# Pairs of four-block transposes of the attention probabilities issued as one visit of TensorE, and a new table of priorities

## The chip, the cores and the metric

The kernel runs on one core of a Trainium2 chip. The metric is the time of the whole program on the device in microseconds (us), as the median of the runs shown. The profile is one execution of the program, taken by the hardware profiler. Engines are named as in the profile: PE (TensorE's matmuls), PEld (its weight loads), DVE (VectorE), ACT (ScalarE), POOL (GpSimd) and SP (the queue that issues nearly all DMAs).

## What is computed

One hybrid decoder layer for a sequence of 2048 tokens and a model width of 1024, in float32. Cut to what matters here:

```python
h = rmsnorm(x, norm_pre_g)
z = einsum('bsd,de->bse', h, w_in)               # 1024 -> 4096 columns
q, k, v, g_attn, c_h, c_b, c_c, g_conv = split(z)
q, k = rope(q), rope(k)                          # 12 heads of 64
for window, dilation in ((128, 1), (512, 4), (2048, 16)):
    o_i, lse_i = dilated_window_attn(q, k, v, window, dilation)
o = sum(softmax(lse) * o_i)                      # mixed by the softmax denominators
attn_out = o * silu(g_attn)
conv_out = c_b * causal_depthwise_conv(c_c * c_h, conv_w) * silu(g_conv)
y = einsum('bse,ed->bsd', concat(attn_out, conv_out), w_out)
out = x + rmsnorm(y, norm_post_g)
```

## The kernel before

The 2048 tokens are cut into four blocks of 512. The input projection runs in 8 groups of 512 columns: groups 0 and 7 feed the convolution, groups 1 to 6 feed one pair of heads each. A group and a block together are a unit; 24 of the 32 units are attention units (`attn_unit`; in the text "the third unit" is the third of these 24, that is pair 0, block 2). Every float32 product is made as three products of rounded parts (`w.ap[:, 0]`, `w.ap[:, 1]`: main part and rest), so a projection step is the three matmuls L933 to L935 into one PSUM bank `z`.

An attention unit does the following. Rotary and scaling on DVE and POOL (L623, L627) with halves swapped by DMA (L611). Scores in two kinds, 4 (the dilated windows) and 1 (the near window): L691 and L719 multiply on halves of 64 rows of TensorE, two heads side by side, into banks `st`. DVE adds the mask and takes the row extreme (L698 for kind 4, L726 for kind 1), ACT takes the exponential (L702, L730). The probabilities `p` then lie with queries on partitions and must be transposed 128 by 128 for the product with v. `parts(h, kind, blk)` does that for up to four blocks: TensorE transposes them into one bank `st` (L759, a matmul against the identity in `cst`), ACT casts the bank to the main part (L764), DVE subtracts to get the rest (L765); both go to one of three buffers `pt`. `times` multiplies by v (L781), `gather` evacuates the result (L797 to L799). For kind 1, and for kind 4 in the first two blocks, a head has 4, 7 or 8 blocks; the loop calls `parts` on four blocks, then `times`, then `parts` on the next four. In the blocks 2 and 3 the far part of kind 4 is transposed on DVE (L750) instead, and the near part, four blocks at a time, as above.

The two kinds are weighted by their softmax denominators: the extremes and sums `e` travel to DRAM and back by small DMAs (L847 `ed<-e`, L849 `ex<-ed`), and DVE begins the weights with L857 to L859 (called the weights step below) as soon as its queue comes to them and `ex` has landed.

The order on every engine is made on the host by `Plan`: each operation has an engine, an estimated duration, a priority and the tiles it reads and writes; `schedule` plays the program through and each engine takes the ready operation of lowest priority number. Operations of TensorE have a mode (0 plain, 1 scores, 2 transposes); while an engine is in mode 1 or 2, a ready operation with a mode is taken before a plain one, so transposes that are ready together are issued together anyway. `SHIFT` moves the priority of single groups of operations, by stage and place in the code. The engines then execute their instructions strictly in this order, so an instruction that waits holds back all that stands behind it on its engine.

The banks are 3 named `z` and 5 named `st`; `st` serves scores, transposes and products with v alike. The loop that the change rewrites:

```python
for i in range(0, len(bl), 4):
    where = parts(h, kind, bl[i:i + 4])
    for half in range(2):
        part = {ac: v for ac, v in where.items() if ac[0] // 2 == half}
        if part:
            times(h, kind, part, O[half])
```

Of the kernel before, what the change touches and what calls it, by code (L numbers as in the profile page):

```python
# [32 lines left out]
ALU = mybir.AluOpType  # L33
# [77 lines left out]
class Op:  # L111
# [3 lines left out]


SHIFT = {
# [5 lines left out]
}  # L123


# [205 lines left out]
def hybrid_layer(ctx: ExitStack, tc: tile.TileContext, x, w_in, w_out, conv_w, g_pre, g_post,  # L331
# [257 lines left out]
    def attn_unit(n, p, b, zs):  # L589
# [144 lines left out]
                    ps + [(P[h, 1], "hold") for h in range(2)], rest)  # L734


        def parts(h, kind, blk, far=False):
            pt, m, pp = Tok(pt_r), len(blk), P[h, kind]
            tiles = sorted({a for a, _ in blk})
            if far:  # L740

                def src():
                    return pp.ap[:, tiles[0]:tiles[-1] + 1, 0:(b - 1) * 128]

                def dst(l):
                    return pt.ap[:, :m, l].rearrange("p (a c) q -> p a c q", c=b - 1)

                def cut(a):
                    return a.rearrange("p a (c q) -> p a c q", q=128)
                add("DVE", dvet(m * 128) + 0.05, pr, lambda: vec.transpose(src(), src()), w=[(pp, a) for a in tiles])  # L750
                add("ACT", actt(m * 128), pr + URG, lambda: act.copy(dst(0), cut(src())), r=[(pp, a) for a in tiles], w=[(pt, 0)])
                add("DVE", dvet(m * 128), pr + URG, lambda: vec.tensor_tensor(dst(1), cut(src()), f(dst(0)), op=ALU.subtract),
                    r=[(pp, a) for a in tiles] + [(pt, 0)], w=[(pt, 1)], port=True)
            else:
                ps = Tok(st_r)

                def tr():
                    for i, (a, c) in enumerate(blk):
                        nc.tensor.transpose(ps.ap[:, i * 128:(i + 1) * 128], pp.ap[:, a, c * 128:(c + 1) * 128], ident)  # L759
                add("PE", 0.111 * m, pr, tr, r=[(pp, a) for a in tiles] + ["cst"], w=[ps, (pt, "hold")], mode=2)  # L760

                def p4():
                    return ps.ap[:, :m * 128].rearrange("p (i c) -> p i c", c=128)
                add("ACT", actt(m * 128, True), pr + URG, lambda: act.copy(pt.ap[:, :m, 0, :], p4()), r=[ps], w=[(pt, 0)])  # L764
                add("DVE", dvet(m * 128), pr + URG, lambda: vec.tensor_tensor(  # L765
                    pt.ap[:, :m, 1, :], p4(), f(pt.ap[:, :m, 0, :]), op=ALU.subtract), r=[ps, (pt, 0)], w=[(pt, 1)])
            return {ac: (pt, i) for i, ac in enumerate(blk)}


# [43 lines left out]
        for kind in (4, 1):  # L813
            for h in range(2):
                if kind == 4:
                    bl = [(r, j) for r in range(4) for j in range(b + 1)]
                else:
                    bl = [(g, s) for g in range(4) for s in range(2) if not (b == 0 and g == 0 and s == 0)]
                if h == 0:
                    UU[kind] = Tok(uu_r), Tok(uu_r)  # L820
                O = [Tok(st_r), Tok(st_r)]
                if kind == 4 and b > 1:
                    where = {}
                    for half in range(2):
                        rs = range(2 * half, 2 * half + 2)
                        if b == 3 or half == 0:
                            where.update(parts(h, 4, [(r, c) for r in (rs if b == 3 else range(4)) for c in range(b - 1)], True))
                        where.update(parts(h, 4, [(r, c) for r in rs for c in (b - 1, b)]))
                        times(h, 4, {ac: v for ac, v in where.items() if ac[0] in rs}, O[half])
                else:  # L830
                    for i in range(0, len(bl), 4):
                        where = parts(h, kind, bl[i:i + 4])
                        for half in range(2):
                            part = {ac: v for ac, v in where.items() if ac[0] // 2 == half}
                            if part:
                                times(h, kind, part, O[half])
                for half in range(2):
                    gather(h, kind, half, O[half])
                if h == 1:
                    a, t = UU[kind]  # L840
                    add("POOL", poolt(C), pr, lambda a=a, t=t: pool.tensor_tensor(a.ap, a.ap, t.ap, op=ALU.add), r=[t], w=[a], port=True)  # L841
# [364 lines left out]
```

## Time and profile before

| what | number |
|---|---|
| median of three runs | 1198.13 us (1196.64 to 1198.43) |
| the profiled execution: its time, its span from first to last instruction | 1198.13 us, 1196.3 us |
| PE busy, matmuls | 1182.5 us (99%), 6716 |
| PEld busy | 981.9 us (82%) |
| DVE busy | 922.5 us (77%) |
| ACT busy | 716.1 us (60%) |
| POOL busy | 265.2 us (22%) |
| DMA queue q1's packets, share of 16 engines | 72.3% |

The busy time of PE overstates its work: a matmul's record includes the pipeline's depth, so records overlap. The work is better read from the distance between the starts of two matmuls that follow each other. The profiled execution took as long as the median of the runs.

### The profile page before, as it was taken

What the parts mean: (1) busy time and instruction counts of PE and PEld (TensorE: products, weight loads), DVE (VectorE), ACT (ScalarE), POOL (GpSimd) and SP (SyncE); (2) the same over time, 40 slices, a digit from 0 to 9 for tenths busy, and PEclk for the clock granted to TensorE, in tenths of its full rate; (3) what the DMA queues carried; (4) which work ended last, traced back from release to release, by engine and by line L of the source; (5) the groups of instructions that cost most, each with busy time, mean ns of one, the idle gap of its engine ahead of it and who ended that gap; (6) DMA issues with size and microseconds to landing.
All of it is one profiled execution on the core that took longest, in us unless ns stands there. A gap on an engine that the chain in (4) does not pass through costs nothing.

```text
span 1196.3 us, 20842 instructions
## 1 busy us (share of the span) xinstructions
PE 1182.5 (99%) x6716; PEld 981.9 (82%) x6716; DVE 922.5 (77%) x2331; ACT 716.1 (60%) x1875; POOL 265.2 (22%) x212
## 2 busy tenths in 40 slices
PE   9999999999999999999999999999999999999997
PEld 7788888888888888888878888888888888888886
DVE  4665478787779977786878867798877899787876
ACT  7433457656757676675857766576767563454443
POOL 0011123322223232222332232232332213100000
PEclk9999999999999999999999999999999999999999
DMA  9989766786768867777768777778657978635452
GB/s 342 371 324 360 247 217 213 251 245 221 213 212 261 255 203 238 215 239 216 231 214 246 235 217 228 222 250 274 225 168 228 318 225 335 203 124 192 139 172 89
DMA packets 175294, 280.46 MB, mean 234 GB/s; under 512 B 53712, under 2 KB 109776, under 8 KB 175184
## 3 DMA queue, kind: packets, MB, share of 16 engines
q1 hardware_dynamic: 174896, 278.86, 72.3%
q8 instruction: 53, 0.87, 0.3%
q14 instruction: 57, 0.47, 0.1%
q10 hardware_dynamic: 288, 0.27, 0.1%
HBM read 215.42 MB, written 51.05 MB: 223 GB/s over the span
## 4 chain that ended last, share of the span: by engine, by line
PE 87%; DMA 5%; DVE 3%; ACT 2%; issue 1%; SPq 1%; DVEq 0%; ACTq 0%
PE z L933 17%; PE z L935 16%; PE z L934 16%; PE st L781 8%; PE st L759 5%; PE st L691 4%; PE st L719 3%; PE st L1100 3%; PE st L1099 3%; PE st L1101 3%; PE z L1101 2%; PE z L1099 2%; PE z L1100 2%; DMA ex<-ed 1%; PE st L933 1%
## 5 line engine op out<-in xcount | busy, mean ns | idle before, releaser
L933 PE MATMUL z<-xt,w 128*128 128x512 f32 x960 | 391.0, 407 | 0.7 <-DVE rp L558 0.4
L935 PE MATMUL z<-xt,w 128*128 128x512 f32 x960 | 376.1, 392 | 0.0
L934 PE MATMUL z<-xt,w 128*128 128x512 f32 x960 | 375.5, 391 | 0.2 <-DVE xt L493 0.2
L933 PEld LDWEIGHTS z<-xt,w 128*128 128x128 f32 x960 | 180.7, 188 | 39.4 <-issue 7.5
L935 PEld LDWEIGHTS z<-xt,w 128*128 128x128 f32 x960 | 180.1, 188 | 39.9
L934 PEld LDWEIGHTS z<-xt,w 128*128 128x128 f32 x960 | 180.9, 188 | 29.7 <-DVE xt L493 0.5
L702 ACT ACTIVATE p<-p,sm 128x128 f32<-128x128 f32 (+3 forms) x192 | 105.7, 553 | 64.1 <-DVE sm L698 64.1
L781 PEld LDWEIGHTS st<-pt,v 128*128 128x128 f32 x852 | 118.2, 190 | 17.4 <-DVE pt L765 4.5
L781 PE MATMUL st<-pt,v 128*128 128x256 f32 x852 | 128.1, 286 | 3.4 <-DVE pt L765 3.2
L765 DVE TENSOR_TENSOR pt<-st,pt 128x512 fp32r<-128x512 f32 (+1 forms) x180 | 116.7, 675 | 16.6 <-ACT pt L764 14.9
L799 DVE TENSOR_TENSOR uu<-st,uu 64x256 f32<-64x256 f32 x192 | 79.5, 420 | 58.4 <-ACT uu L798 44.9
L797 ACT COPY uu<-st 64x256 f32<-64x256 f32 x192 | 69.5, 367 | 66.0 <-PE st L781 55.8
L764 ACT CAST pt<-st 128x512 fp32r<-128x512 f32 (+1 forms) x180 | 98.3, 579 | 14.6 <-PE st L759 12.1
L841 POOL TENSOR_TENSOR uu<-uu 128x512 f32<-128x512 f32 x48 | 69.3, 1443 | 158.8 <-DVE uu L799 139.3
L730 ACT ACTIVATE p<-p,e 128x256 f32<-128x256 f32 (+1 forms) x192 | 94.7, 497 | 15.8 <-DVE e L726 15.8
L698 DVE CUSTOM_DVE_ANT_0 p<-st,cst 128x128 f32<-128x128 f32 (+3 forms) x192 | 81.9, 486 | 28.1 <-PE st L691 27.7
L759 PE MATMUL st<-cst,p 128*128 128x128 f32 x708 | 98.3, 273 | 0.0
L759 PEld LDWEIGHTS st<-cst,p 128*128 128x128 f32 x708 | 82.5, 140 | 11.8 <-issue 1.2
L623 POOL TENSOR_TENSOR rp<-rp,cs 128x512 f32<-128x512 f32 x24 | 36.2, 1509 | 216.7 <-DMA rp<-rp 96.0
L798 ACT COPY uu<-st 64x256 f32<-64x256 f32 x192 | 68.7, 367 | 18.6 <-PE st L781 13.2
L726 DVE CUSTOM_DVE_ANT_0 p<-st,cst 128x256 f32<-128x256 f32 (+1 forms) x192 | 66.9, 410 | 13.9 <-PE st L719 13.6
L623 DVE TENSOR_TENSOR rp<-rp,cs 128x512 f32<-128x512 f32 x72 | 53.8, 764 | 20.4 <-DMA rp<-rp 18.8
(315 smaller groups left out, 1912.7 us busy)
## 6 DMA issues: line engine op xcount, KB each, us to landing
xt<-xt SPq DMA_DIRECT2D x256, 512.0 KB
cs<-t SPq DMA_DIRECT2D x28, 768.0 KB
raw<-in_w_in SPq DMA_DIRECT2D x58, 256.0 KB
rp<-rp SPq DMA_DIRECT2D x192, 64.0 KB
vd<-v SPq DMA_DIRECT2D x24, 512.0 KB
v<-vd SPq DMA_DIRECT2D x96, 128.0 KB
ab<-ad SPq DMA_DIRECT2D x48, 256.0 KB
uu<-mix SPq DMA_DIRECT2D x27, 256.0 KB
```

The source lines that it names most:

```text
L623: add(e, dur, pr, lambda o=o, a=a, i=i, eng=eng: eng.tensor_tensor(o.ap, a.ap, cs.ap[:, i], op=ALU.mult), r=[cs], w=[o], port=True)
L698: add("DVE", dvet(w) + 0.01, pr + URG, lambda h=h, r=r, P4=P4: vec.tensor_tensor_reduce(P4.ap[:, r, 0:w], ps[h].ap[:, (r - r0) * w:(r - r0 ...
L702: add("ACT", actt(w) + 0.19, pr, lambda h=h, r=r, P4=P4: act.activation(P4.ap[:, r, 0:w], P4.ap[:, r, 0:w], AF.Exp, bias=s4(0, h)[:, r:r + ...
L730: add("ACT", actt(256 - lo[g]) + 0.19, pr, lambda h=h, g=g, P1=P1: act.activation(P1.ap[:, g, lo[g]:], P1.ap[:, g, lo[g]:], AF.Exp, bias=E ...
L759: nc.tensor.transpose(ps.ap[:, i * 128:(i + 1) * 128], pp.ap[:, a, c * 128:(c + 1) * 128], ident)
L764: add("ACT", actt(m * 128, True), pr + URG, lambda: act.copy(pt.ap[:, :m, 0, :], p4()), r=[ps], w=[(pt, 0)])
L765: add("DVE", dvet(m * 128), pr + URG, lambda: vec.tensor_tensor(pt.ap[:, :m, 1, :], p4(), f(pt.ap[:, :m, 0, :]), op=ALU.subtract), r=[ps, ...
L781: mm(dst, v, pt.ap[:, i], start=s, stop=e)
L799: add("DVE", dvet(256), pr + URG, lambda: vec.tensor_tensor(cols(a, lo), o()[lo:lo + 64, 0], cols(a, lo), op=ALU.add), r=[O], w=[(a, (h, h ...
L933: mm(z.ap, w.ap[:, 0, js], xt.ap[:, 0], start=kt == 0, stop=False)
L934: mm(z.ap, w.ap[:, 0, js], xt.ap[:, 1], start=False, stop=False)
L935: mm(z.ap, w.ap[:, 1, js], xt.ap[:, 0], start=False, stop=kt == KT - 1)
```

## The change

`parts` gets a flag `last`. It no longer adds its TensorE operation at once: it collects it in `turn`, and the call with `last=True` adds one operation that transposes all collected blocks, into as many banks and `pt` buffers as there are calls. The casts and subtractions are collected likewise in `splits` and follow. In the loop above, all calls of a head come first, with `last` on the final one, and the products with v come after. Calls of `parts` elsewhere (blocks 2 and 3 of kind 4) have `last=True` and are as they were. The table `SHIFT` has other entries. No instruction is added or removed on TensorE, and 180 casts and 180 subtractions stay.

```diff
 SHIFT = {
-    (-1, 15): 90, (1, 24): -3, (5, 70): 10, (6, 69): 60, (7, 50): 30, (8, 50): 30, (9, 66): -3, (11, 43): 20,
+    (-1, 15): 90, (1, 24): -3, (5, 46): -60, (5, 52): 3, (5, 70): 10, (7, 22): -30, (7, 44): -30, (9, 68): -60,
...
-        def parts(h, kind, blk, far=False):
+        turn, splits = [], []
+
+        def parts(h, kind, blk, far=False, last=True):
             pt, m, pp = Tok(pt_r), len(blk), P[h, kind]
...
                 def tr():
                     for i, (a, c) in enumerate(blk):
                         nc.tensor.transpose(ps.ap[:, i * 128:(i + 1) * 128], pp.ap[:, a, c * 128:(c + 1) * 128], ident)
-                add("PE", 0.111 * m, pr, tr, r=[(pp, a) for a in tiles] + ["cst"], w=[ps, (pt, "hold")], mode=2)
+                turn.append((0.111 * m, tr, [(pp, a) for a in tiles], [ps, (pt, "hold")]))
+                if last:
+                    parts_of = list(turn)
+                    add("PE", sum(v[0] for v in parts_of), pr, lambda: [v[1]() for v in parts_of],
+                        r=[k for v in parts_of for k in v[2]] + ["cst"], w=[k for v in parts_of for k in v[3]], mode=2)
+                    turn.clear()
 
                 def p4():
                     return ps.ap[:, :m * 128].rearrange("p (i c) -> p i c", c=128)
-                add("ACT", actt(m * 128, True), pr + URG, lambda: act.copy(pt.ap[:, :m, 0, :], p4()), r=[ps], w=[(pt, 0)])
-                add("DVE", dvet(m * 128), pr + URG, lambda: vec.tensor_tensor(
-                    pt.ap[:, :m, 1, :], p4(), f(pt.ap[:, :m, 0, :]), op=ALU.subtract), r=[ps, (pt, 0)], w=[(pt, 1)])
+                def split():
+                    add("ACT", actt(m * 128, True), pr + URG, lambda: act.copy(pt.ap[:, :m, 0, :], p4()), r=[ps], w=[(pt, 0)])
+                    add("DVE", dvet(m * 128), pr + URG, lambda: vec.tensor_tensor(
+                        pt.ap[:, :m, 1, :], p4(), f(pt.ap[:, :m, 0, :]), op=ALU.subtract), r=[ps, (pt, 0)], w=[(pt, 1)])
+                splits.append(split)
+                if last:
+                    for fn in splits:
+                        fn()
+                    splits.clear()
...
-                    for i in range(0, len(bl), 4):
-                        where = parts(h, kind, bl[i:i + 4])
+                    wheres = [parts(h, kind, bl[i:i + 4], last=i + 4 >= len(bl)) for i in range(0, len(bl), 4)]
+                    for where in wheres:
```

In the changed code the lines from L759 on have higher numbers: the transpose L759 is L761, the cast L764 is L772, the subtraction L765 is L773, the product L781 is L794, the evacuation L797 to L799 is L810 to L812, the weights step L857 is L870, and the projection L933 to L935 is L946 to L948.

Three places show how the instructions move. First, PE in the first attention unit, where the second head's seven blocks of kind 1 (`p11`) are transposed. Names are tile and buffer number; `pt` are the transposed probabilities, `v10` the values, `z` the projection's banks. Before:

```order
L759 MATMUL st1_118<-cst_65,p11_188 128x128 x4
L933 MATMUL z0_114<-xt4_126,w4_135 128x512
L934 MATMUL z0_114<-xt4_126,w4_135 128x512
L935 MATMUL z0_114<-xt4_126,w4_135 128x512
L781 MATMUL st4_121<-pt2_191,v10_176 128x2x128 x3
L781 MATMUL st3_120<-pt2_191,v10_176 128x2x128
L781 MATMUL st3_120<-pt0_189,v10_176 128x2x128 x3
L759 MATMUL st2_119<-cst_65,p11_188 128x128 x3
```

The same place after the change:

```order
L794 MATMUL st1_118<-pt2_191,v10_176 128x2x128 x3
L794 MATMUL st3_120<-pt2_191,v10_176 128x2x128
L794 MATMUL st3_120<-pt0_189,v10_176 128x2x128 x3
L761 MATMUL st2_119<-cst_65,p11_188 128x128 x4
L761 MATMUL st4_121<-cst_65,p11_188 128x128 x3
L946 MATMUL z1_115<-xt6_128,w5_136 128x512
```

The two visits of four and three have become one of seven, into two banks, and it stands behind the first head's products. Counted through the whole order, runs of transposes that follow each other without another matmul between go from 154 to 141 (the 180 calls of `parts`, the transposes of v and of x together); runs of four go from 93 to 61, runs of eight from 30 to 58. Runs of score matmuls are 60 in both.

Second, DVE in the third unit, around its weights step (`sm0<-ex0` is its first instruction). Before:

```order
L799 TENSOR_TENSOR uu_149<-st1_118,uu_149 64x256
L857 TENSOR_TENSOR sm0_161<-ex0_155,sm2_163 128x8
L858 TENSOR_TENSOR sm0_161<-sm0_161,ex0_155 128x8
L859 TENSOR_TENSOR sm0_161<-sm0_161,sm2_163 128x8
L799 TENSOR_TENSOR uu_149<-st2_119,uu_149 64x256
L765 TENSOR_TENSOR pt1_190<-st3_120,pt1_190 128x4x128
L799 TENSOR_TENSOR uu_149<-st4_121,uu_149 64x256
L615 TENSOR_TENSOR rp0_142<-z2_116,cs0_192 128x512
```

And after:

```order
L773 TENSOR_TENSOR pt1_190<-st2_119,pt1_190 128x4x128
L773 TENSOR_TENSOR pt0_189<-st4_121,pt0_189 128x4x128
L528 SCALAR_TENSOR_TENSOR g2_148<-rp1_143,g2_148 128x512
L870 TENSOR_TENSOR sm0_161<-ex0_155,sm2_163 128x8
L871 TENSOR_TENSOR sm0_161<-sm0_161,ex0_155 128x8
L872 TENSOR_TENSOR sm0_161<-sm0_161,sm2_163 128x8
L662 TENSOR_TENSOR v23_174<-st0_117,v23_174 128x4x64 x2
L812 TENSOR_TENSOR uu_149<-st1_118,uu_149 64x256
```

The subtraction for `pt` that stood behind the weights step now stands ahead of it, as one of a pair.

Third, DVE in the nineteenth unit (pair 4, block 2), the same step. Before:

```order
L765 TENSOR_TENSOR pt2_191<-st4_121,pt2_191 128x4x128
L857 TENSOR_TENSOR sm0_161<-ex0_155,sm2_163 128x8
L858 TENSOR_TENSOR sm0_161<-sm0_161,ex0_155 128x8
L859 TENSOR_TENSOR sm0_161<-sm0_161,sm2_163 128x8
L799 TENSOR_TENSOR uu_149<-st3_120,uu_149 64x256
L662 TENSOR_TENSOR v22_173<-st2_119,v22_173 128x4x64
L765 TENSOR_TENSOR pt1_190<-st0_117,pt1_190 128x4x128
```

And after (`p40<-st0` and the rows like it are the masks on the next unit's scores, L698):

```order
L528 SCALAR_TENSOR_TENSOR g1_147<-rp2_144,g1_147 128x512
L870 TENSOR_TENSOR sm0_161<-ex0_155,sm2_163 128x8
L871 TENSOR_TENSOR sm0_161<-sm0_161,ex0_155 128x8
L872 TENSOR_TENSOR sm0_161<-sm0_161,sm2_163 128x8
L812 TENSOR_TENSOR uu_149<-st3_120,uu_149 64x256
L698 ISA p40_182,sm1_162<-st0_117,cst_65 128x512
L698 ISA sm1_162 128x1
L698 ISA p41_183,sm1_162<-st4_121,cst_65 128x512
```

The weights step has come to stand directly ahead of an evacuation and of the next unit's masks.

8 rows, old and new, of the table SHIFT are left out of this document.

## The prediction

> **What bounds the kernel now.** I read the page first, its engines and the chain that ended last, then idle time of PE by stretch, then the starts of single matmuls around a visit of transposes, then the waits of PE.
>
> ```profile
> PE 1182.5 (99%) x6716; PEld 981.9 (82%) x6716; DVE 922.5 (77%) x2331; ACT 716.1 (60%) x1875; POOL 265.2 (22%) x212
> PE 87%; DMA 5%; DVE 3%; ACT 2%; issue 1%; SPq 1%; DVEq 0%; ACTq 0%
> L781 PE MATMUL st<-pt,v 128*128 128x256 f32 x852 | 128.1, 286 | 3.4 <-DVE pt L765 3.2
> L765 DVE TENSOR_TENSOR pt<-st,pt 128x512 fp32r<-128x512 f32 (+1 forms) x180 | 116.7, 675 | 16.6 <-ACT pt L764 14.9
> L764 ACT CAST pt<-st 128x512 fp32r<-128x512 f32 (+1 forms) x180 | 98.3, 579 | 14.6 <-PE st L759 12.1 <-DVE pt L765 0.9
> L759 PE MATMUL st<-cst,p 128*128 128x128 f32 x708 | 98.3, 273 | 0.0
> ```
>
> PE is the bound: 87% of the chain that ended last is PE's own work. The transposes L759 never found PE idle (0.0 in the last column), the products L781 for 3.4 us in all. The attention units lie between 130 and 990 us; the next view is the busy time of all engines in two halves of that stretch (length first, then PE).
>
> ```profile
> 130.00:560.00 430.00, 427.80 (x2612) 357.17 (x2612) 335.30 (x909) 283.28 (x790) 118.65 (x97) 1.00 0.76 235
> 560.00:990.00 430.00, 427.48 (x2615) 356.86 (x2615) 346.78 (x929) 288.55 (x803) 122.18 (x96) 1.00 0.75 232
> ```
>
> PE is idle for 2.2 and 2.5 us there, 4.7 us of 860. So two things can change the time: what the visits cost in PE's own stream, and how much PE waits. At 99% busy the first would count in full.
>
> **What a visit costs.** From the timeline of PE (start, length; the length overlaps, so only starts count): a visit of four transposes, then one of eight.
>
> ```profile
> 261.73 0.40 PE L935 MATMUL z<-xt,w 128*128 128x512 f32 x1
> 261.96 0.60 PE L759 MATMUL st<-cst,p 128*128 128x128 f32 x4
> 262.32 0.48 PE L933 MATMUL z<-xt,w 128*128 128x512 f32 x1
> 262.64 0.39 PE L934 MATMUL z<-xt,w 128*128 128x512 f32 x1
> 262.87 0.40 PE L935 MATMUL z<-xt,w 128*128 128x512 f32 x1
> ...
> 274.13 1.03 PE L759 MATMUL st<-cst,p 128*128 128x128 f32 x8
> 274.93 0.48 PE L933 MATMUL z<-xt,w 128*128 128x512 f32 x1
> 275.25 0.39 PE L934 MATMUL z<-xt,w 128*128 128x512 f32 x1
> ```
>
> A projection matmul takes 0.23 us from start to start (262.64 to 262.87). Entering costs nothing: 261.73 to 261.96 is also 0.23. From the first of four transposes to the second projection matmul are 0.68 us; less one matmul at 0.23, the visit cost 0.45. For eight: 1.12 less 0.23, that is 0.89. So four transposes more cost 0.44, 0.11 each, and two visits of four cost 0.90 where one of eight costs 0.89. One visit saved is worth 0.01 us, with the rounding of these starts at most 0.03. The matmul after the transposes starts early (0.36 after the first of four, where four would take 0.44) and the next one late (0.32 in place of 0.23); the two nearly cancel.
>
> **The change part by part.**
>
> *Fewer visits.* 180 calls of `parts` would make 120 operations, which sounds like 60 visits less. But the old planner already put ready transposes side by side, and in the whole order there are only 13 runs less (154 to 141). 13 x 0.01 is 0.13 us, at most 0.4; even 60 would be 0.6. I take 0.13. No product with v, no transpose, no score visit is added or removed; casts (180 x 0.58) and subtractions (180 x 0.68) stay and lie on ACT (60% busy) and DVE (77%).
>
> *What a change of mode could cost.* The nearest other row is a score visit, which works on halves of 64 rows:
>
> ```profile
> 287.19 0.39 PE L935 MATMUL z<-xt,w 128*128 128x512 f32 x1
> 287.51 1.56 PE L691 MATMUL st<-kk,q 64*128 64x128 f32 x24
> ...
> 289.78 0.51 PE L933 MATMUL z<-xt,w 128*128 128x512 f32 x1
> 290.12 0.40 PE L934 MATMUL z<-xt,w 128*128 128x512 f32 x1
> ```
>
> Entering takes 0.32 and leaving 0.34 in place of 0.23 each, 0.20 us per visit. That is the upper bound for a visit of any kind; with it the 13 visits would be 2.6 us. The trace shows the transposes themselves at 0.01, and there are 60 score visits before and after, so the sum keeps 0.13. The Trainium skill has the rule behind this price, in TensorEngine Tiling (Array Packing), Key Properties: a change of the tiling mode drains TensorE. The score visits agree with it; a transpose of whole 128 by 128 tiles stays in the one-tile mode, and the trace agrees that it pays almost nothing.
>
> *Pairs instead of singles.* The product with v needs cast and subtraction of its bank. For the second bank of a pair that is two casts and a subtraction, 0.58 + 0.58 + 0.68 = 1.84 us with nothing else on ACT and DVE. Counted in the orders with 0.23 per projection matmul, 0.11 per transpose and 0.12 per product, the least work of PE between a visit's end and the first product that uses it is 2.7 us before and 2.5 us after, and half the sites have about 3.7 in both. So the cover is there, by 0.7 us at the tightest place; if DVE is late by more than that, PE stands. A pair also takes two of five `st` banks and two of three `pt` at once, so the next pair must wait for the products of the first; the order lets projections run meanwhile. I cost this at nothing, between 0 and what the first rival gives.
>
> *The new order.* This is the term that decides. The waits of PE, in total, number and longest:
>
> ```profile
> PE st L781 <- DVE pt L765: 3.2, 4, 1.5
> PE st L655 <- DVE rp L615: 1.3, 1, 1.3
> ...
> 615.85 1.04 DVE L857 TENSOR_TENSOR sm<-ex,sm 128x8 f32<-128x8 f32 x1 [0.34 <-DMA ex<-ed]
> 618.77 0.69 DVE L615 TENSOR_TENSOR rp<-z,cs 128x512 f32<-128x512 f32 x1
> ...
> L857 DVE TENSOR_TENSOR sm<-ex,sm 128x8 f32<-128x8 f32 x24 | 8.1, 337 | 9.9 <-DMA ex<-ed 9.6
> ```
>
> The row of 1.3 us is the fourteenth unit, where L615 came behind that unit's weights step on DVE (the two rows of the timeline). Over all 24 units DVE waited 9.6 us for `ex` (last row).
>
> The longest is in the third unit. There the queue SP issued eight `rp` transfers and `mix` before the four `ed`; `ex` went out at 229.71, and DVE stood at the weights step until it landed, with the subtraction for a product of PE behind it:
>
> ```profile
> 217.19 5.01 SPq L611 DMA_DIRECT2D rp<-rp  x8
> 222.87 2.50 SPq L847 DMA_DIRECT2D ed<-e  x4
> 229.71 0.37 SPq L849 DMA_DIRECT2D ex<-ed  x1
> ...
> 210.30 1.84 PE L719 MATMUL st<-kk,q 64*128 64x256 f32 x24
> 236.11 0.71 PE L781 MATMUL st<-pt,v 128*128 128x256 f32 x4 [1.52 <-DVE pt L765]
> ...
> 234.59 0.17 DVE L857 TENSOR_TENSOR sm<-ex,sm 128x8 f32<-128x8 f32 x1 [3.39 <-DMA ex<-ed]
> 235.29 0.67 DVE L765 TENSOR_TENSOR pt<-st,pt 128x512 fp32r<-128x512 f32 x1
> ```
>
> `ex` needed 4.9 us to land (229.71 to 234.59), 22.5 us after the unit's last score visit ended (212.14). Between that visit and the first PE work that needs DVE behind the weights step the old order had 63 projection matmuls, 38 transposes and 36 products: 14.5 + 4.2 + 4.3 = 23.0 us. The new order has 78, 41 and 32, that is 26.3 us, and the subtraction stands ahead of the step. So this stall of 1.5 us goes. What is late next there is the evacuation and the copy of v, which the 26.3 us cover.
>
> In the nineteenth unit it is the other way round: the cushion was 57, 41 and 36 (21.9 us) and is 45, 24, 20 and one score visit (1.9 us), 17.3 us.
>
> ```profile
> 774.45 1.84 PE L719 MATMUL st<-kk,q 64*128 64x256 f32 x24
> 789.15 0.37 SPq L849 DMA_DIRECT2D ex<-ed  x1
> 792.50 1.09 DVE L857 TENSOR_TENSOR sm<-ex,sm 128x8 f32<-128x8 f32 x1
> 794.02 0.42 DVE L799 TENSOR_TENSOR uu<-st,uu 64x256 f32<-64x256 f32 x1 [0.15 <-ACT uu L798]
> ```
>
> The visit ended at 776.29, the step began 16.2 us later and the evacuation behind it ended 18.2 us later, 0.9 past the new cushion. If `ex` lands sooner than the step asked for it, nothing is lost; with 4.9 us from 789.15 it lands 17.8 us after the visit, the evacuation ends at about 18.6, and 1.3 us are lost. I take the middle, 0.7 us. The same count over all 24 units gives a mean cushion of 21.9 before and 20.9 after; those under 19 us go from 3 to 6. So I take: the two long waits (1.5 and 1.3, the second also behind a weights step, whose cushion grows from 21 to 23 us) go, and about as much comes back in several small ones, 0.7 to 1 us at three or four places. Sum: nothing.
>
> *Start, end and DMAs.* The order starts alike on all engines up to the attention units, and the output stage has the same instructions; moved DMAs of the 24 units are covered as above. Nothing.
>
> The profiled execution took 1198.13 us, 1.8 us more than its span of 1196.3 us, and is itself the median of the runs. 1198.13 - 0.13 and no sum of waits: **1198.0 us**.
>
> **How it could go otherwise.**
>
> *Waits behind the weights step grow (slower).* With its cushion at 17 to 19 us in six units and a landing as in the third unit, each loses up to 1.3 us, and the masks for the next unit's scores, which now stand right behind the step, are late too. Six times 1.0, less 1.5 for the third unit: 4.5 us, 1202.5 us. It decides from a landing about 17 us after the score visit on. Against it: before, the step's 24 waits for `ex` were 9.6 us together, 0.4 each.
>
> *Pairs run out of cover (slower).* 48 pairs have 2.5 us or more against 1.84; POOL and DVE can hold each other up. If DVE is late by 1 us at a tenth of the pairs, 3 to 4 us: 1201.5 us. For it: products already waited for the subtraction four times.
>
> *The waits go and none come (faster).* The ceiling is all idle time of PE, 4.7 us, and what the overlap hides: records are 0.39 long at a pitch of 0.23, so 0.16 per wait. The two long waits alone are 2.8 us with 0.3 hidden: 1194.9 us.
>
> *Visits cost as much as score visits (faster).* 13 x 0.20 is 2.6: 1195.5 us. The trace speaks against it. By the page named above that would be right only if a transpose changed the tiling mode.
>
> **The numbers.** A change within 0.2% (2.4 us) is what a measurement of this kernel can't tell from none. Forecast 0.40; weights step 0.20, pairs 0.11; waits gone 0.25, visit price 0.04. So faster 0.29, same 0.40, slower 0.31. The forecast's own range is 1195.7 to 1200.4. The whole range goes up past the two slower cases to 1204.0, and down past the faster ones to 1193.0, where all of PE's idle time in the attention units (4.7 us) would be gone; below and above I leave out about 1 in 10 each.
>
> **What would show it.** The starts around a visit of eight transposes as above, 0.89 us; the busy time of PE within 2 us of 1182.5; no wait of the third unit at its weights step; small waits of L794 for L773, or of PE for an evacuation or a mask, in the seventh, fifteenth or nineteenth unit. The prediction is wrong if PE's idle time between 130 and 990 us is under 2 or over 7.5 us, or if the price of a visit differs from 0.01 by more than 0.03.

## The result: 18 us slower, and the loss is in the output stage

The changed kernel takes 1216.04 us as the median of three runs (1214.66 to 1216.39). The ratio to the kernel before is 1.0147, with a 95% interval of 1.0131 to 1.0164. The forecast was 1198.0 us and its range ended at 1204. The profiled execution has a span of 1212.9 us where the kernel before had 1196.3, so 16.6 us are to be found in the trace.

From the page of the changed kernel: the engines, the slices of PE and of the clock granted to it, and the chain that ended last.

```profile
PE 1189.1 (98%) x6716; PEld 985.2 (81%) x6716; DVE 914.5 (75%) x2331; ACT 714.8 (59%) x1875; POOL 256.0 (21%) x212
PE   9999999999999999999999999999999999699997
...
PEclk9999999999999999999999999999999999799999
...
PE 83%; DMA 6%; DVE 5%; ACT 3%; issue 1%; SPq 1%; POOL 0%; DVEq 0%; ACTq 0%; POOLq 0%
```

One slice of PE holds a 6 and the same slice of the clock a 7; in the kernel before both rows hold 9 there. A slice is 30 us, so this one begins at about 1031 us, behind the attention units. The two halves of the attention stretch, in the view shown for the kernel before:

```profile
130.00:560.00 430.00, 428.58 (x2598) 357.68 (x2597) 330.74 (x891) 278.11 (x777) 117.45 (x97) 1.00 0.75 237
560.00:990.00 430.00, 429.37 (x2617) 358.91 (x2616) 330.13 (x915) 278.14 (x780) 115.70 (x96) 1.00 0.73 230
```

PE is idle there for 1.4 and 0.6 us, 2.0 us where it was 4.7. So the stretch on which the prediction rested became a little better. Now the same view for 1030 to 1060 and 1060 to 1100 us, first of the kernel before:

```profile
1030.00:1060.00 30.00, 30.00 (x131) 24.21 (x131) 25.23 (x49) 14.86 (x30) 3.24 (x2) 1.00 0.48 150
1060.00:1100.00 40.00, 40.00 (x174) 32.27 (x173) 33.08 (x71) 18.30 (x42) 0.00 (x0) 1.00 0.50 165
```

and of the changed kernel:

```profile
1030.00:1060.00 30.00, 19.60 (x62) 14.59 (x63) 24.81 (x39) 12.19 (x21) 4.13 (x3) 0.77 0.44 138
1060.00:1100.00 40.00, 37.32 (x157) 28.54 (x156) 33.81 (x72) 20.59 (x44) 0.00 (x0) 1.00 0.54 172
```

PE starts 131 matmuls in the first of these stretches before, and 62 after; in the second 174 and 157. These are 86 matmuls of 512 columns fewer. At 0.233 us from start to start, the distance of the output matmuls, that is 20.0 us. The last projection comes 3.6 us earlier than before (below), so 16.4 of the 16.6 us are accounted for. The waits of PE name the place (total, number, longest):

```profile
PE st L1112 <- ACT xt L1080: 7.1, 2, 3.9
PE st L1114 <- DVE xt L1081: 3.5, 1, 3.5
PE st L794 <- DVE pt L773: 1.5, 3, 0.8
```

L1112 to L1114 are the output projection's three matmuls (L1099 to L1101 before). `xt` is their left operand: rows of the mixed layer output, cast by ACT (L1080) and reduced to the rest by DVE (L1081). The waits at L1112 and L1114 were not there before. Here are the last product with v, the last projection and the start of the output stage, from PE's timeline of the kernel before:

```profile
983.06 0.63 PE L781 MATMUL st<-pt,v 128*128 128x256 f32 x4
...
1032.99 0.39 PE L935 MATMUL z<-xt,w 128*128 128x512 f32 x1
1033.21 0.39 PE L1099 MATMUL st<-kk,xt 128*128 128x512 f32 x1
```

and of the changed kernel:

```profile
1014.38 1.11 PE L794 MATMUL st<-pt,v 128*128 128x256 f32 x8
...
1029.43 0.39 PE L948 MATMUL st<-xt,w 128*128 128x512 f32 x1
1033.73 0.50 PE L1112 MATMUL st<-kk,xt 128*128 128x512 f32 x1 [3.92 <-ACT xt L1080]
1034.08 0.39 PE L1113 MATMUL st<-kk,xt 128*128 128x512 f32 x1
1037.92 0.80 PE L1114 MATMUL st<-kk,xt 128*128 128x512 f32 x1 [3.46 <-DVE xt L1081]
1038.52 0.63 PE L1112 MATMUL st<-pt,xt 128*128 128x512 f32 x1
1038.94 0.63 PE L1113 MATMUL st<-pt,xt 128*128 128x512 f32 x1
...
1045.33 0.80 PE L1112 MATMUL st<-kk,xt 128*128 128x512 f32 x1 [3.21 <-ACT xt L1080]
```

Before, the attention ends 50 us ahead of the last projection; 219 projection matmuls are left for PE, counted in the order. After, it ends 15 us ahead, with 63 left. Between 130 and 990 us PE was hardly ever short of work (2.0 us idle): it did the projections earlier, in place of attention work that was not ready in the plan. The attention units fall behind slowly. The last score visit of the thirteenth and of the last unit, before:

```profile
570.26 1.04 PE L719 MATMUL st<-kk,q 64*128 64x256 f32 x12
...
953.60 1.87 PE L719 MATMUL st<-kk,q 64*128 64x256 f32 x24
```

and after:

```profile
590.66 1.04 PE L719 MATMUL st<-kk,q 64*128 64x256 f32 x12
...
982.66 1.87 PE L719 MATMUL st<-kk,q 64*128 64x256 f32 x24
```

The visits of the first unit begin within 0.1 us of each other in both; these come 20 and 29 us later. That is 1.3 us for each unit on average, 1.7 in the first half and 0.8 in the second.

What happens in those 50 us is the preparation of the output weights: 128 by 512 pieces are loaded from `w_out`, most are combined with others on DVE (L989 before, L1002 after), cast on ACT (L1005, L1018) and reduced to the rest on DVE (L1006, L1019). The forms are kept in buffers of the attention (`kk`, `q`, `v2`, `pt`, `v1`), which this line hands over: `kk` and `q` when the last scores are done, the rest when the last product with v is done:

```python
gates = [gated(early, score_last + w_last, lambda: None), gated(later + anew[0], attn_last + w_last, lambda: layout(0))]
```

A second rule hangs on the same hand-over. In the code the loads of the left operands (`uu<-mix`) are put behind the eighth load from `w_out` (`after=loads[7:8]`), and that load belongs to the part that waits for the attention's end. The first load of a left operand goes out, in the kernel before and in the changed one, at

```profile
1013.76 1.59 SPq L1060 DMA_DIRECT2D uu<-mix  x3
...
1024.72 0.38 SPq L1073 DMA_DIRECT2D uu<-mix  x1
```

In DVE's timeline the first left operand then comes behind weights' sums and rests and behind the last convolution unit's work. Before it stands at

```profile
1022.67 1.50 DVE L1068 TENSOR_TENSOR xt<-uu,xt 128x512 fp32r<-128x512 f32 x2
```

that is 10 us ahead of the last projection, and after at

```profile
1037.18 0.69 DVE L1081 TENSOR_TENSOR xt<-uu,xt 128x512 fp32r<-128x512 f32 x1
```

8 us behind it. On ACT its cast stands directly behind an instruction of the convolution unit (L527), which waited for DVE:

```profile
1032.54 0.63 ACT L527 ACTIVATE rp<-g 128x512 f32<-128x512 f32 x1 [3.74 <-DVE g L526]
1033.08 0.60 ACT L1080 CAST xt<-uu 128x512 fp32r<-128x512 f32 x1
```

### The profile page after: what moved, and what is told of

Read it like the earlier page. It is cut to its first block, busy times and chain, and to the rows that moved or that the text cites. A ratio compares the mean times of both kernels' runs of the same rounds, so it can differ in the third digit from the quotient of the medians.

```text
span 1212.9 us, 20823 instructions
## 1 busy us (share of the span) xinstructions
PE 1189.1 (98%) x6716; PEld 985.2 (81%) x6716; DVE 914.5 (75%) x2331; ACT 714.8 (59%) x1875; POOL 256.0 (21%) x212
## 4 chain that ended last, share of the span: by engine, by line
PE 83%; DMA 6%; DVE 5%; ACT 3%; issue 1%; SPq 1%; POOL 0%; DVEq 0%; ACTq 0%; POOLq 0%
PE z L946 16%; PE z L948 15%; PE z L947 15%; PE st L794 8%; PE st L761 5%; PE st L691 4%; PE st L719 3%; PE st L1114 2%; PE st L1112 2%; PE st L1113 2%; DMA ex<-ed 2%; PE z L1113 2%; PE z L1114 2%; PE z L1112 2%; DMA ed<-e 1%
## 5 line engine op out<-in xcount | busy, mean ns | idle before, releaser
L946 PE MATMUL z<-xt,w 128*128 128x512 f32 x960 | 391.5, 408 | 0.3 <-DVE u L559 0.3
L948 PE MATMUL z<-xt,w 128*128 128x512 f32 x960 | 376.1, 392 | 0.4 <-DVE w L451 0.4
L948 PEld LDWEIGHTS z<-xt,w 128*128 128x128 f32 x960 | 180.1, 188 | 40.6 <-DVE w L451 0.8
L946 PEld LDWEIGHTS z<-xt,w 128*128 128x128 f32 x960 | 180.8, 188 | 39.1 <-issue 6.9
L812 DVE TENSOR_TENSOR uu<-st,uu 64x256 f32<-64x256 f32 x192 | 79.1, 420 | 82.8 <-ACT uu L811 70.1
L810 ACT COPY uu<-st 64x256 f32<-64x256 f32 x192 | 70.0, 367 | 109.4 <-PE st L794 98.7
L773 DVE TENSOR_TENSOR pt<-st,pt 128x512 fp32r<-128x512 f32 (+1 forms) x180 | 116.1, 674 | 21.0 <-ACT pt L772 19.6
L794 PEld LDWEIGHTS st<-pt,v 128*128 128x128 f32 x852 | 117.0, 190 | 15.4 <-DVE pt L773 4.4
L794 PE MATMUL st<-pt,v 128*128 128x256 f32 x852 | 123.2, 284 | 1.7 <-DVE pt L773 1.5
L854 POOL TENSOR_TENSOR uu<-uu 128x512 f32<-128x512 f32 x48 | 64.6, 1345 | 262.1 <-DVE uu L812 227.1
L772 ACT CAST pt<-st 128x512 fp32r<-128x512 f32 (+1 forms) x180 | 97.3, 578 | 13.6 <-PE st L761 12.6
L730 ACT ACTIVATE p<-p,e 128x256 f32<-128x256 f32 (+1 forms) x192 | 94.5, 497 | 11.6 <-DVE e L726 11.4
L761 PE MATMUL st<-cst,p 128*128 128x128 f32 x708 | 96.0, 273 | 0.0
L698 DVE CUSTOM_DVE_ANT_0 p<-st,cst 128x128 f32<-128x128 f32 (+3 forms) x192 | 81.8, 486 | 17.7 <-PE st L691 17.4
L761 PEld LDWEIGHTS st<-cst,p 128*128 128x128 f32 x708 | 81.9, 140 | 9.9 <-issue 0.9
L623 DVE TENSOR_TENSOR rp<-rp,cs 128x512 f32<-128x512 f32 x72 | 58.8, 835 | 21.1 <-DMA rp<-rp 19.8
L643 POOL CAST q<-q 128x512 fp32r<-128x512 f32 x48 | 33.9, 720 | 123.6 <-PE st L719 89.9
```

Of the source, the lines that this page charges most:

```text
L698: add("DVE", dvet(w) + 0.01, pr + URG, lambda h=h, r=r, P4=P4: vec.tensor_tensor_reduce(P4.ap[:, r, 0:w], ps[h].ap[:, (r - r0) * w:(r - r0 ...
L730: add("ACT", actt(256 - lo[g]) + 0.19, pr, lambda h=h, g=g, P1=P1: act.activation(P1.ap[:, g, lo[g]:], P1.ap[:, g, lo[g]:], AF.Exp, bias=E ...
L794: mm(dst, v, pt.ap[:, i], start=s, stop=e)
L810: add("ACT", actt(256, True) + HALF / 2, pr + URG, lambda: act.copy(cols(a, lo), o()[hi:hi + 64, 0]), r=[O], w=[(a, (h, half))])
L812: add("DVE", dvet(256), pr + URG, lambda: vec.tensor_tensor(cols(a, lo), o()[lo:lo + 64, 0], cols(a, lo), op=ALU.add), r=[O], w=[(a, (h, h ...
L946: mm(z.ap, w.ap[:, 0, js], xt.ap[:, 0], start=kt == 0, stop=False)
```

## The experiments

Theory A: pairs hold two of the three `pt` buffers, so in the plan the next transposes of a head wait for products. Each attention unit ends later, projections fill PE meanwhile, and when they are used up the preparation of the output weights has too little work of PE beside it. Theory B: the new table causes the loss. A third, C, came up later: the weights' preparation is innocent, and the first products wait because the last attention rows themselves come late. The ratios are against runs of the kernel before beside the kernel's own. In the table "left" is the number of projection matmuls behind the last product with v, counted in the order; the output stage is the time from the start of the last projection to the end of the span.

| kernel | left | last product, us | output stage, us | median, us | ratio (95%) |
|---|---|---|---|---|---|
| before | 219 | 983 | 163.3 | 1198.1 | 1 |
| changed | 63 | 1014 | 183.5 | 1216.0 | 1.0147 (1.0131 to 1.0164) |
| before, new table | 231 | 983 | 163.7 | 1202.2 | 1.0040 (1.0026 to 1.0053) |
| changed, old table | 27 | 1039 | 192.1 | 1240.7 | 1.0362 (1.0339 to 1.0386) |
| changed, 4 `pt`, 8 `xt` | 249 | 991 | 168.4 | 1215.6 | 1.0144 (1.0120 to 1.0168) |
| changed, 3 `pt`, 8 `xt` | 51 | 1039 | 183.8 | 1237.3 | 1.0335 (1.0307 to 1.0362) |
| before, 2 `pt` | 81 | 1033 | 180.1 | 1233.2 | 1.0306 (1.0283 to 1.0329) |
| changed, pairs for kind 4 only | 249 | 974 | 163.3 | 1195.9 | 0.9988 (0.9977 to 0.9999) |
| changed, pairs for kind 1 only | 75 | 1018 | 185.3 | 1222.3 | 1.0211 (1.0194 to 1.0228) |
| changed, 4 `pt`, 2 `v1` | 270 | 972 | 163.3 | 1200.7 | 1.0024 (1.0013 to 1.0035) |
| before, second hand-over late | | 980 | 178.0 | 1210.5 | 1.0122 (1.0104 to 1.0140) |
| before, both hand-overs late | | 979 | 172.5 | 1204.6 | 1.0063 (1.0048 to 1.0078) |

**The two halves of the change apart.** One kernel is the one before with the new `SHIFT`, the other the changed one with the old `SHIFT`.

> The kernel before with the new SHIFT table and nothing else; 231 projection matmuls are left after the last product with v (219 before, 63 in the changed kernel). Theory A (pairs take two of three pt buffers, the attention units fall behind, the projections are used up and PE stands at the start of the output stage): 1196 to 1201 us, PE's idle time after 1010 us as before. Theory B (the new table is what is slow): about 1216 us, with 10 us or more of idle PE at the start of the output stage.

> The changed kernel with the SHIFT table of before; 27 projection matmuls are left after the last product. Theory A: slower than the changed kernel, since 36 matmuls less (8 us) cover the preparation of the output weights: 1219 to 1226 us, more idle PE after 1010 us than the 13 us there. Theory B: about 1198 us.

The new table alone costs 0.4%, and with it the output stage stays at 163.7 us. The pairs with the old table cost 3.6%, more than A expected, with only 27 matmuls left and one wait of 22.6 us at L1112. So the pairs make the loss, and the new table takes back more than half of it; B falls.

**Are the `pt` buffers the reason?** A fourth `pt` needs room, so an `xt` buffer is given up, and the control gives up the `xt` alone.

```diff
-    xp_r = ring(cp, "xt", 9, [128, 2, C], F32R, "STREAM")
+    xp_r = ring(cp, "xt", 8, [128, 2, C], F32R, "STREAM")
-    pt_r = ring(ap_, "pt", 3, [128, 4, 2, 128], F32R)
+    pt_r = ring(ap_, "pt", 4, [128, 4, 2, 128], F32R)
```

> The changed kernel with four pt buffers in place of three (an xt buffer is given up for the room: eight in place of nine); 249 projection matmuls are left after the last product. Theory A: the loss is gone, 1195 to 1200 us, and the last product comes at about 985 us in place of 1015. Theory B: still about 1216 us, since the table is the new one.

> Control for the run with four pt buffers: the changed kernel with eight xt buffers in place of nine and three pt; 51 projection matmuls are left after the last product. Theory A: 1216 to 1221 us, as the changed kernel or a little slower. If it were the xt buffer that mattered: about 1198 us.

The waits of PE with 8 `xt` and 3 `pt`:

```profile
PE st L794 <- DVE pt L773: 12.2, 11, 2.6
PE st L1112 <- ACT xt L1080: 11.4, 3, 5.4
```

and with 8 `xt` and 4 `pt`:

```profile
PE st L655 <- DVE rp L615: 4.5, 6, 1.3
PE z L946 <- DMA xt<-xt: 4.1, 3, 2.1
PE st L794 <- DVE pt L773: 3.8, 7, 1.9
PE z L1112 <- ACT xt L1080: 2.4, 1, 2.4
```

The lost `xt` buffer costs far more than either expectation allowed, so the absolute times miss; the 1215.6 us with four `pt` are even the time that B named. The comparison of the two holds: one `pt` more is worth 21.7 us, moves the last product 48 us forward and shortens the wait at L1112 from 11.4 us to 2.4. Part of what the lost `xt` costs lies in other places: the second kernel waits for `xt` and `rp` ahead of the output stage.

The same from the other side: the kernel before with two `pt` buffers, no pairs.

```diff
-    pt_r = ring(ap_, "pt", 3, [128, 4, 2, 128], F32R)
+    pt_r = ring(ap_, "pt", 2, [128, 4, 2, 128], F32R)
```

> The kernel before, single visits and its old table, with two pt buffers in place of three: what a pair takes is here taken away outright. 81 projection matmuls are left after the last product. Theory A (too few pt buffers lengthen the attention units, the last product comes late, PE stands at the start of the output stage): 1208 to 1220 us, last product at about 1010 us instead of 983, 5 us or more of idle PE at the start of the output stage. Rival (pairs as such, or their two PSUM banks, do the harm, not the pt buffers): 1196 to 1202 us.

```profile
PE st L1099 <- ACT xt L1067: 8.4, 3, 6.8
...
PE st L1101 <- DVE xt L1068: 3.9, 2, 2.6
```

The pattern of the changed kernel appears without any pair: late attention, the same waits at the first output matmuls. The size was missed again, to the upper side (PE also idles for 14.6 us of 850 in the attention stretch).

Last, room for the fourth `pt` taken from `v1` instead of `xt` (`v1` 2 in place of 3):

> The changed kernel with four pt buffers, the room taken from the v1 buffers (two in place of three) and xt left at nine. 270 projection matmuls are left after the last product. Theory A: 1194 to 1202 us, last product by 990 us, no wait over 2 us at the start of the output stage; with pairs and the new table both still there. If pairs are harmful whatever the buffers: 1210 us or more.

All pairs are there, the output stage is back at 163.3 us and the loss shrinks from 1.5% to 0.2%. The time lies in A's range. What is left is no more than the new table costs without pairs (0.4%), and the two intervals overlap.

**Which pairs?** The 48 pairs of kind 1 or the 12 of kind 4:

```diff
-                    wheres = [parts(h, kind, bl[i:i + 4], last=i + 4 >= len(bl)) for i in range(0, len(bl), 4)]
+                    wheres = [parts(h, kind, bl[i:i + 4], last=kind == 1 or i + 4 >= len(bl)) for i in range(0, len(bl), 4)]
```

(the other kernel has `kind == 4` there).

> The changed kernel with pairs only for kind 4 of the second block (12 of the 60 pairs); kind 1 is visited singly, four blocks at a time, but both visits stand ahead of the products in the code. 249 projection matmuls are left after the last product. Theory A: 1195 to 1203 us, last product at about 980 us. If the pairs of any kind cost per visit, in proportion to their number: about 1202 us.

> The changed kernel with pairs only for kind 1 (48 of the 60). 75 projection matmuls are left after the last product. Theory A: 1211 to 1222 us, last product at about 1012 us, PE idle for 8 us or more at the start of the output stage.

The pairs of kind 1 make the loss. With pairs for kind 4 only, 249 matmuls are left, and this is the one version with a ratio below 1, by 0.1%; the interval's end is 0.9999, so it hardly differs from the kernel before. A cost in proportion to the number of pairs (about 1202 us) is out. Does that time hang on the table?

> Pairs only for kind 4 (12 of the 60 pairs), as in the run of 1195.9 us, with the table of the kernel before. 225 projection matmuls are left after the last product (219 before, 249 with the new table). Theory A: more than 200 are left, so the output stage stays at 163 to 164 us and the time at 1195 to 1199 us. Rival (the table is what makes the pairs pay): 1200 us or more.

It took 1203.35 us, 1.0059 (1.0044 to 1.0074). The output stage is 163.7 us, as A says for 225 matmuls left, but the time is not what A expected from that; it is the rival's. The attention itself is slower with the old table: between 130 and 980 us PE is idle for 9.3 us, against 3.3 with the new one.

**Is the short cover the cause, or the late attention?** In the kernel before, with attention untouched, the hand-over of the weights' buffers is put off until only some projections are left. `projs` lists the 1024 projection steps, so `projs[:-1024]` is empty.

```diff
+              projs.append(done)
...
-    gates = [gated(early, score_last + w_last, lambda: None), gated(later + anew[0], attn_last + w_last, lambda: layout(0))]
+    gates = [gated(early, score_last + w_last + projs[:-1024], lambda: None), gated(later + anew[0], attn_last + w_last + projs[:-21], lambda: layout(0))]
```

> The kernel before (singles, its own table, three pt buffers), with one edit: the buffers of the attention that hold the second part of the output weights' forms (v2, pt, v1) are handed over only when 21 projection steps (63 matmuls, 14 us) are left, as many as are left after the last product in the kernel with pairs; the first part (kk, q) is handed over as before. No attention unit, no pair and no pt wait is touched. Theory A (the loss sits in the output weights, prepared with too little work of TensorE beside them): the last projection stays near 1033 us, VectorE is full with the forms (L1006, L989) behind it, and the output stage takes 170 to 183 us instead of 163, so 1205 to 1217 us. Theory C (the first products wait for the last attention unit's own rows, which come 32 us later in the kernel with pairs, and the weights' preparation is only beside it): those rows are as early as before, so 1197 to 1200 us.

> The kernel before with both parts of the buffers handed over late: the first part (kk, q) when 71 projection steps (213 matmuls, about 49 us) are left, the second (v2, pt, v1) when 35 (105 matmuls, about 24 us) are left. Theory A: milder than with 63 matmuls left, 1200 to 1210 us, the output stage 166 to 176 us. Theory C: 1197 to 1200 us.

Of the kernel with the second hand-over late: the waits, then PE and the clock in the slices of the page, then the window.

```profile
PE st L1102 <- DVE xt L1069: 7.8, 1, 7.8
PE st L1100 <- ACT xt L1068: 1.8, 1, 1.8
```

```profile
PE   9999999999999999999999999999999999699997
...
PEclk9999999999999999999999999999999999799999
```

```profile
1030.00:1060.00 30.00, 20.44 (x72) 15.47 (x71) 25.42 (x40) 13.38 (x24) 3.62 (x3) 0.77 0.44 140
```

The two rows of slices read as those of the changed kernel, though the attention ends at 980 us and there is no pair. The output stage is 14.7 us longer, and the time 13.7 us: the late hand-over alone makes such a loss, as A says, and C's time did not come. The code speaks against C too: the first output products read the rows of block 0, whose last attention unit is the twenty-first and not the last; its last score visit begins at 873.6 us in the changed kernel. With more cover for the second part (105 matmuls), though the first part is late as well, the loss is 7.8 us.

One thing this edit doesn't separate. It puts off the weights and, by the rule on the eighth load, the left operands with them: the first of these loads goes out at 1022.18 us here. No run takes that rule away, so how much of the loss is the weights' work and how much the late start of the operands' loads is not shown.

**What is the share of the clock?** Behind the stands of 3.92 and 3.46 us the matmuls follow each other by 0.43 us instead of 0.23, and the window's granted clock is 0.77. I filled the stands with matmuls of the identity, first twice too long, then fitting.

```diff
+                    def idle(n, t):
+                        for _ in range(n):
+                            mm(t.ap[:, 0:128], ident, ident, start=True, stop=True)
+                    if q0 and e == 0 and at < 2:
+                        idle((32, 26)[at], z)
...
+                    if q0 and e == 0 and at == 0:
+                        idle(28, bank1)
```

> The changed kernel, with 86 matmuls of the identity by itself (128x128) put into the three stands of TensorE at the start of the output stage: 32 ahead of the first product (3.5 us by 0.109 us each, in a stand of 3.9), 28 ahead of its third matmul (3.1 in 3.5), 26 ahead of the second bank's first (2.8 in 3.2). Their sums are overwritten. If the pitch of 0.43 us behind these stands (0.23 elsewhere) is the clock that is lowered after a stand, the products run at 0.23 to 0.25 us a matmul and the time falls by 3 to 5 us, to 1211 to 1213 us. If the pitch comes from something else (traffic of VectorE and the DMAs at the buffers), it stays at 0.43 and the time at 1215 to 1217 us.

The trace has two records of 0.114 us for each of these matmuls, so 19.7 us were filled where the stands were 10.6, and the kernel took 1219.05 us, ratio 1.0184 (1.0169 to 1.0199). The expected gain is missed, but all matmuls behind the fillings ran at 0.23 us and the clock of the whole execution was 0.999. With 16, 14 and 13 of them:

> The changed kernel with 16, 14 and 13 matmuls of the identity (0.228 us each as measured in pair_idlework: 3.65, 3.19 and 2.96 us) put into the three stands of 3.92, 3.46 and 3.21 us. In the changed kernel the matmuls behind the stands ran at a pitch of 0.43 us instead of 0.23: 1038.52 to 1041.72 and 1045.33 to 1051.74 us, some 21 matmuls by 0.2, 4 to 5 us. If that is the clock, the pitch is 0.23 there and the time 1211 to 1213 us; if the clock's loss is taken up by later waits for VectorE, the pitch is 0.23 and the time 1214 to 1216 us.

From PE's timeline of this kernel, behind the second and at the third filling:

```profile
1038.90 0.50 PE L1122 MATMUL st<-kk,xt 128*128 128x512 f32 x1 [0.32 <-DVE xt L1081]
1039.24 0.40 PE L1118 MATMUL st<-pt,xt 128*128 128x512 f32 x1
1039.47 0.39 PE L1119 MATMUL st<-pt,xt 128*128 128x512 f32 x1
...
1041.34 3.07 PE L1115 MATMUL st<-cst 128*128 128x128 f32 x26
1046.31 0.50 PE L1118 MATMUL st<-kk,xt 128*128 128x512 f32 x1 [1.91 <-ACT xt L1080]
...
1047.47 0.80 PE L1122 MATMUL st<-kk,xt 128*128 128x512 f32 x1 [0.25 <-DVE xt L1081]
1048.07 0.63 PE L1118 MATMUL st<-v,xt 128*128 128x512 f32 x1
1048.49 0.63 PE L1119 MATMUL st<-v,xt 128*128 128x512 f32 x1
```

The first bank's products run at 0.23. But what they gain is then waited for: the third wait, for `xt`, was 3.2 us and is 3.07 of filling and 1.9 of wait. The time is 1214.76 us, 1.0147 (1.0125 to 1.0170), no different from the changed kernel. In the changed kernel the slow clock lengthens PE's own rows by some 4.6 us (about 22 matmuls by 0.2). At the first bank this is a consequence: the left operands set the pace there. At the second bank the matmuls were slow in this run too, so what the clock costs there was not tested.

**Is it VectorE?** The 16 sums of the weights shrunk to 16 columns:

```diff
-            combine(at(name), C, lambda: o.ap, lambda: a.ap, lambda: b.ap, ALU.subtract, o, [k for k in (a, b) if k is not o])
+            combine(at(name), 16, lambda: o.ap[:, :16], lambda: a.ap[:, :16], lambda: b.ap[:, :16], ALU.subtract, o, [k for k in (a, b) if k is not o])
```

> The changed kernel with the 16 sums of the output weights (L1002, less) made on 16 of their 512 columns, so each takes about 0.07 us instead of the 0.60 us by which they follow each other: 8 to 9 us less of VectorE between 1016 and 1051 us, the weights left unsummed. Loads, casts, hand-over of buffers and attention are as they were. If VectorE is what the first products wait for, most of that comes back, with some of the clock: 1203 to 1210 us. If it is the loads or the hand-over of the buffers, 1213 to 1217 us.

1211.54 us, ratio 1.0117 (1.0099 to 1.0136). It lies between the two expectations: 4.5 us of the 18 come back, not 6 to 13. The wait is still there:

```profile
PE st L1112 <- ACT xt L1080: 8.6, 1, 8.6
```

That VectorE's sums are a part of what the first products wait for is likely and not shown. The shorter sums changed the plan too: the first load of a left operand goes out at 1031.43 us, where it was 1024.72, and its cast on ACT now stands behind a later instruction of the convolution unit (L573). How the loss splits between the sums, the casts on ACT, the loads, the last convolution unit's work on DVE, which stands in the same queue, and the order in which they follow each other stays open.

## Why the prediction was wrong, step by step

- **Fewer visits, 0.13 us: right in its price.** A visit of eight in the changed kernel:

```profile
278.84 1.03 PE L761 MATMUL st<-cst,p 128*128 128x128 f32 x8
279.63 0.48 PE L946 MATMUL z<-xt,w 128*128 128x512 f32 x1
279.95 0.39 PE L947 MATMUL z<-xt,w 128*128 128x512 f32 x1
```

  1.11 us less 0.23 are 0.88; 0.89 was foretold. The rival with the price of a score visit is out with it.
- **"So the cover is there, by 0.7 us at the tightest place": right.** L794 waits for L773 three times, 1.5 us in all, where it was four times and 3.2.
- **"A pair also takes two of five `st` banks and two of three `pt` at once ... the order lets projections run meanwhile. I cost this at nothing": this step failed.** What it says happened: projections ran meanwhile and PE did not stand. But a projection spent there is missing later. It should have been counted to the end of the order: 219 projection matmuls behind the last product before, 63 after. The number was to be had from the order ahead of any run.
- **"Start, end and DMAs ... the output stage has the same instructions ... Nothing": this step failed too.** The instructions are the same, their cover is not. The term that was put at nothing is 20 us in the output stage, less 3.6 for the earlier last projection.
- **The new order.** The long wait of the third unit is gone, as foretold: its weights step began at 235.41 us with no wait for `ex`. The cushions of the others did shrink: over all 24 units DVE's waits for `ex` grew from 9.6 to 29.5 us. PE did not feel it; its idle time in the stretch fell from 4.7 to 2.0 us, which at 2.05 is just inside the 2 us set as the bound. So the rival "waits behind the weights step grow" had its cause and not its effect, and the rival "the waits go and none come" was right in direction for that stretch and wrong in the sum. The table alone, without pairs, still costs 0.4%; where, no run took apart.
- **PE's busy time** was to stay within 2 us of 1182.5 and is 1189.1. No matmul was added: records behind the stands are 0.63 long in place of 0.39.

None of the rivals was the case that came. All looked inside the stretch in which the change is made.

## What to carry to other kernels

If an engine at 99% fills its gaps with work that is ready at any time, that work is a stock. Count in the order how much of it is left when the late part of the program needs cover: here an output stage that took 163 to 168 us with 219 or more matmuls left took 180 to 192 with 27 to 81. Look also at what the loads of the late part are made to wait for. Before two steps are joined, count the buffers that the joined step holds, and for how long; with three buffers a step that takes two leaves no room for a second such step.

## What the runs showed of the hardware

The clock was lowered by short stands. After 3.92 us it held for one more matmul; after a further 3.46 us the matmuls ran at 0.43 us from start to start, for 3.6 us; after a stand of 3.21 us they ran so for about 6 us. The granted clock of the 30 us around was 0.77. The Trainium skill, TensorE: Matmul & The Clock Gate, Part 1, states an idle window of about 3.4 us for that, and about as long a busy one to come back. The changed kernel agrees for the stand of 3.46 us and the 3.6 us behind it, not for the 3.21 us and the 6 us. In the kernel with the fitting fillings the matmuls ran at 0.42 to 0.43 us behind a wait of 1.91 us and one of 0.25 us as well, so here the length of one stand alone did not decide. A matmul of the identity by itself took 0.228 us in two records, twice what a transpose of the same size took (0.11).
